# Sample attention of a hybrid decoder step: four sequences' scores side by side on the tensor engine, keys transposed a quarter at a time

## The chip, the core and the metric

One core of a Trainium2 chip runs the whole kernel in one launch. The metric is the device time of a launch in microseconds (us), as the median of three runs. The engines are named as the profile names them: PE is the tensor engine's matrix multiply, PEld its weight load, DVE the vector engine, ACT the scalar engine, POOL the GpSimd engine, and SP the sync engine, which here only issues transfers (DMAs).

## What is computed

One step of a one-layer decoder for a prompt (512 positions) and for a sample group (8 sequences of 8 new positions, with 256 cached positions behind each). The part that matters here is the sample group's windowed attention. It has three head groups with window and dilation (128,1), (512,4) and (2048,16), each with 4 heads of width 64. Cut to the core, the reference does this for each head group, with `q` the normalised queries:

```python
def dilated_cached_attn(q, k_all, v_all, d, n_past):
    T = q.shape[1]
    idx = n_past + jnp.arange(T)[:, None] - d * jnp.arange(BAND + 1)[None, :]
    valid = idx >= 0
    ...
    s = jnp.einsum('bthd,btjhd->bthj', q, kg) * (Dh ** -0.5)
    s = jnp.where(valid[None, :, None, :], s, -jnp.inf)
    m = jnp.max(s, axis=-1, keepdims=True)
    p = jnp.exp(s - m)
    den = jnp.sum(p, axis=-1, keepdims=True)
    o = jnp.einsum('bthj,btjhd->bthd', p / den, vg)
    return o, (m + jnp.log(den))[..., 0]
```

The three groups' results are then merged by softmax weights over their log-denominators. A softmax over all three groups' keys at once gives the same, and that is how the kernel does it: of each sequence it needs 128 keys of the first cache, 256 of the second and 128 of the third (the rows that the dilation can reach), so 512 cached keys, and the new keys behind them.

## The kernel before

**The whole.** The program is a chain of projections on PE with everything else woven between. Each projection is cut into groups: a group of `feat_groups` is 24 matmuls into a tile `pf` (lines 191 to 193), a group of `tok_groups` is 24 matmuls into a tile `ptok` (lines 956 to 958), or 16 for the sample tokens (lines 952 and 953). Weights come in by a DMA from SP into `raw` (line 160), are split by ACT into a high part `wh` (line 138) and by DVE into a low part `wl` (line 139), and go to PE. `Weave.run(main, between)` (line 84) emits the groups of `main` and spreads the steps of the list `between` evenly over the gaps behind them. PE executes in exactly this written order. The orders of DVE, ACT and SP are set by a scheduler when the kernel is built, and each of these engines works through its own list in order: an instruction that waits holds up all that stand behind it.

**The stage of the change.** Line 1023 runs 14 groups (a small low-rank projection, then query, key and value projections of the recurrent branch) with the steps of `sample_steps` between them. Nothing later than this stage reads the sample attention's result before the branches are merged.

**The sample attention.** It works in two halves of four sequences (`half(0)`, `half(1)`). `load_cache` brings a sequence's 512 keys (or values) into a tile `kv` of four quarters of 128 rows x 256 by three DMAs (lines 1296 to 1298: quarter 0, quarters 1 and 2, quarter 3). There are 5 buffers. The steps of a half are:

- `keys(bi)`: loads sequence `bi`'s keys, transposes its 2 x 4 blocks of 128 x 128 on PE into two PSUM tiles `ptk` (line 1311), and copies them to `kTs`, one by DVE and one by ACT (line 1312). `kTs` has 2 buffers.
- `scores(bi)`: the sequence's queries stand in `Qm.Q` as blocks of 32 columns (8 positions x 4 heads). Its scores go to 32 rows of the PSUM tile `psSs`, rows 32*bi and following: six matmuls, two of 256 columns and four of 128 (line 1321). Six more against the new keys go to `psSn` (line 1324). The program puts a matmul of 32 stationary columns on one of four sets of 32 columns of the PE array, by its output rows (0, 32, 64 or 96 and following). So one call of `scores` stays on one set. Behind the fourth sequence follows the softmax of the half: mask additions, maximum, exponential (ACT, line 1334), reciprocal (DVE, line 1335) and scaling (DVE, line 1336) of the tile `Ps`.
- `turn()`: transposes `Ps` (`ptP`, line 1342, and `ptN`, line 1346) and copies it to `PTs` and `PTn`.
- `sums()`: loads the four value tiles and sums the values into `psOs`, one matmul over the new keys (line 1352) and 16 over the cached ones (line 1356). These 16 go around the four column sets: quarter by quarter, and in each quarter sequence by sequence. DVE then masks the sums into `osam` (line 1359).
- `turn_out()`: two small matmuls `ptOs` from `osam` (line 1364), and a split into `aH` and `aL`.

The list of steps that `sample_steps` returns is written by hand:

```python
    return [k0[0], k0[1], s0[0], k0[2], s0[1], k0[3], s0[2], s0[3], k1[0], k1[1], t0, s1[0], k1[2], v0, s1[1],
            k1[3], o0, s1[2], s1[3], rest, rest, t1, rest, v1, rest, o1]
```

Here k, s, t, v and o are keys, scores, turn, sums and turn_out, the digit is the half, and the index is the sequence.

Of the kernel before, what the change touches and what calls it, by code (L numbers as in the profile page):

```python
# [9 lines left out]
F32 = mybir.dt.float32  # L10
# [8 lines left out]
P = 128  # L19
# [881 lines left out]
def sample_masks(E, at):  # L901

    V = E.V
    ms = at.tile([P, NSC], F32, name="msam")
    with E.sb("mka", 2) as wk:
        compare(E, wk, ms[:, 0:128], [[1, 128]], ALU.is_ge, E.p7)
        compare(E, wk, ms[:, 128:384], [[0, 64], [1, 4]], ALU.is_equal, E.p3)
        compare(E, wk, ms[:, 384:512], [[0, 16], [1, 8]], ALU.is_equal, E.p7)
        own = wk.tile([P, 32], F32, tag="own", name="own")
        oth = wk.tile([P, 96], F32, tag="oth", name="oth")  # L910
        compare(E, wk, own, [[1, 4], [0, 8]], ALU.is_equal, E.p5)
        compare(E, wk, oth[:, 0:32], [[0, 4], [1, 8]], ALU.is_le, E.p7)
# [12 lines left out]
    E.ms = ms
# [61 lines left out]
def mixer(E, mxs, bk, xpool, opening):  # L987
# [298 lines left out]
def sample_steps(E, st, Qm):  # L1286

    V, S, G, PE, SP = E.V, E.S, E.G, E.PE, E.SP
    ps_bg, ident = E.ps_bg, E.ident
    wk = st.enter_context(E.sb("samw", 2))  # L1290
    sample_masks(E, Qm.pool)
    cv = [c.rearrange("b r k h d -> b r k (h d)") for c in (E.cache0, E.cache1, E.cache2)]

    def load_cache(b, kv):
        c = wk.tile([P, 4, 256], F32, tag="kv", name="kv", bufs=5)
        SP.dma_start(c[:, 0, :], cv[0][b][:, kv])
        SP.dma_start(c[:, 1:3, :], cv[1][b].rearrange("(c r) k d -> r c k d", r=P)[:, :, kv])
        SP.dma_start(c[:, 3, :], cv[2][b].rearrange("(a r) k d -> a r k d", r=16)[:, 0:8, kv])
        return c

    def half(hf):
        w = SimpleNamespace(k={})
        rn = slice(32 * hf, 32 * hf + 32)

        def keys(bi):
            ck = load_cache(4 * hf + bi, 0)
            w.k[bi] = kTs = wk.tile([P, 2, 512], F32, tag="w4", name="kTs")
            for j in range(2):
                pt = ps_bg("ptk")
                for i in range(4):  # L1310
                    PE.transpose(pt[:, i * P:(i + 1) * P], ck[:, i, j * P:(j + 1) * P], ident)
                (S.copy if j else V.tensor_copy)(kTs[:, j, :], pt)

        def scores(bi):
            b = 4 * hf + bi
            if bi == 0:
                w.S, w.N = ps_bg("psSs"), ps_bg("psSn")
            rr = slice(32 * bi, 32 * bi + 32)
            for (c0, c1, g) in ((0, 128, 0), (128, 384, 1), (384, 512, 2)):
                for j in range(2):  # L1320
                    PE.matmul(w.S[rr, c0:c1], Qm.Q[:, g, j, b, :], w.k[bi][:, j, c0:c1], start=(j == 0), stop=(j == 1))
            for g in range(3):
                for j in range(2):
                    PE.matmul(w.N[rr, g * 32:(g + 1) * 32], Qm.Q[:, g, j, b, :], Qm.K[:, g, j, rn],
                              start=(j == 0), stop=(j == 1))
# [3 lines left out]
            V.tensor_add(Ps[:, :512], w.S, E.ms[:, :512])
# [3 lines left out]
            V.tensor_scalar(st[:, 1:2], st[:, 0:1], -1.0, None, op0=ALU.mult)
            S.activation(Ps, Ps, AF.Exp, bias=st[:, 1:2], accum_out=st[:, 2:3])
            V.reciprocal(st[:, 3:4], st[:, 2:3])
            V.tensor_scalar(Ps, Ps, st[:, 3:4], None, op0=ALU.mult)

        def turn():
            w.T = wk.tile([P, 512], F32, tag="w2", name="PTs")
            pt = ps_bg("ptP")  # L1340
            for i in range(4):
                PE.transpose(pt[:, i * P:(i + 1) * P], w.P[:, i * P:(i + 1) * P], ident)
            S.copy(w.T, pt)
            w.Tn = wk.tile([96, P], F32, tag="PTn", name="PTn", bufs=1)
            pt = ps_bg("ptN")
            PE.transpose(pt[:96, :P], w.P[:, 512:NSC], ident)
            V.tensor_copy(w.Tn, pt[:96, :P])

        def sums():

            po = ps_bg("psOs")
            PE.matmul(po[:, :256], w.Tn, Qm.V[:, hf, :], start=True, stop=False, skip_group_check=True)
            vs = [load_cache(4 * hf + bi, 1) for bi in range(4)]
            for i in range(4):
                for bi in range(4):
                    PE.matmul(po[32 * bi:32 * bi + 32, :256], w.T[:, i * P + bi * 32:i * P + bi * 32 + 32], vs[bi][:, i, :],
                              start=False, stop=(i == 3), skip_group_check=True)
            w.o = wk.tile([P, 256], F32, tag="osam", name="osam")
            V.tensor_mul(w.o, po[:, :256], E.mh)

        def turn_out():
            pt = ps_bg("ptOs")
            for j in range(2):
                PE.matmul(pt[:, 32 * j:32 * j + 32], w.o[:, j * P:(j + 1) * P], E.pick, start=True, stop=True)
            tok = slice(SEQ + 32 * hf, SEQ + 32 * hf + 32)
            E.split(E.aH[:, :, tok], E.aL[:, :, tok], pt[:, 0:64].rearrange("p (j t) -> p j t", j=2))

        f = lambda fn, *a: lambda: fn(*a)
        return [f(keys, b) for b in range(4)], [f(scores, b) for b in range(4)], turn, sums, turn_out

    (k0, s0, t0, v0, o0), (k1, s1, t1, v1, o1) = half(0), half(1)
    rest = lambda: None
    return [k0[0], k0[1], s0[0], k0[2], s0[1], k0[3], s0[2], s0[3], k1[0], k1[1], t0, s1[0], k1[2], v0, s1[1],
            k1[3], o0, s1[2], s1[3], rest, rest, t1, rest, v1, rest, o1]


class Recurrence:
# [349 lines left out]
```

## Time and profile before

| what | us |
|---|---|
| median of 3 runs (lowest, highest) | 1443.35 (1442.48, 1445.37) |
| time of the profiled execution | 1446.7 |
| span of its trace | 1444.2 |
| PE busy | 1414.2 (98% of the span) |
| DVE busy | 1055.3 (73%) |
| ACT busy | 716.7 (50%) |
| the stage of the change, from the first transposed keys to the last `ptOs` | about 629.8 to 700.4 |

The span is the time from the first to the last instruction in the trace; the launch's own time has 2.5 us around it. Rows of the timeline give the start, the time, the engine, the line, the operation, output<-inputs and a count: equal instructions that follow each other are merged in one row, which lasts from the first start to the last end. A float32 matmul shows as two rows of the trace, a transpose as one, so six `scores` matmuls count as x12. Successive PE rows overlap, since a matmul's time includes the way through the array; the pace of PE is read from the distance of the starts.

### The profile page before, as it was taken

What the parts mean: (1) busy time and instruction counts of PE and PEld (TensorE: products, weight loads), DVE (VectorE), ACT (ScalarE), POOL (GpSimd) and SP (SyncE); (2) the same over time, 40 slices, a digit from 0 to 9 for tenths busy, and PEclk for the clock granted to TensorE, in tenths of its full rate; (3) what the DMA queues carried; (4) which work ended last, traced back from release to release, by engine and by line L of the source; (5) the groups of instructions that cost most, each with busy time, mean ns of one, the idle gap of its engine ahead of it and who ended that gap; (6) DMA issues with size and microseconds to landing.
All of it is one profiled execution on the core that took longest, in us unless ns stands there. A gap on an engine that the chain in (4) does not pass through costs nothing.

```text
span 1444.2 us, 27493 instructions
## 1 busy us (share of the span) xinstructions
PE 1414.2 (98%) x10860; PEld 1382.0 (96%) x10860; DVE 1055.3 (73%) x2318; ACT 716.7 (50%) x1458; POOL 66.6 (5%) x105
## 2 busy tenths in 40 slices
PE   7999999999989999999999999999998999999998
PEld 7999999999989999898999999999998999999997
DVE  5999999998845554532576757455579999999882
ACT  6554564665534464622565734223345556556642
POOL 1000000000112211000000000000000000000000
PEclk9999999999999999999999999999999999999999
DMA  7313323332433332274223433235231232333232
GB/s 187 90 43 100 104 84 106 88 103 77 140 107 111 111 120 77 84 204 133 63 74 92 121 110 100 81 95 153 74 88 45 80 111 85 93 104 100 86 106 66
DMA packets 180687, 144.26 MB, mean 100 GB/s; under 512 B 7466, under 2 KB 179168, under 8 KB 180560
## 3 DMA queue, kind: packets, MB, share of 16 engines
q1 hardware_dynamic: 179456, 139.98, 33.4%
q0 software_dynamic: 1104, 2.54, 0.5%
q8 instruction: 85, 1.39, 0.4%
q14 instruction: 42, 0.34, 0.1%
HBM read 128.72 MB, written 13.78 MB: 99 GB/s over the span
## 4 chain that ended last, share of the span: by engine, by line
PE 91%; DVE 5%; DMA 1%; ACT 1%; SPq 1%; issue 0%; POOL 0%; ACTq 0%; POOLq 0%; DVEq 0%
PE pX L545 8%; PE pX L544 7%; PE pX L543 7%; PE pY L545 4%; PE pY L544 4%; PE pY L543 4%; PE pf L191 4%; PE pf L193 3%; PE pf L192 3%; PE ptok L956 3%; PE ptok L958 3%; PE ptok L957 3%; PE pg L191 2%; PE pg L193 2%; PE pg L192 2%; PE pZ L544 2%
## 5 line engine op out<-in xcount | busy, mean ns | idle before, releaser
L138 ACT CAST w<-raw 128x512 fp32r<-128x512 f32 (+1 forms) x348 | 197.9, 577 | 128.5 <-PE pX L545 35.4
L139 DVE TENSOR_TENSOR w<-raw,w 128x512 fp32r<-128x512 f32 (+1 forms) x348 | 215.4, 631 | 18.5 <-ACT w L138 16.3
L138 ACT CAST wh<-raw 128x1024 fp32r<-128x1024 f32 (+2 forms) x115 | 110.7, 972 | 120.2 <-PE pf L192 38.2
L545 PE MATMUL pX<-hop,w 128*128 128x288 f32 x544 | 162.1, 298 | 4.3 <-DVE w L139 4.3
L139 DVE TENSOR_TENSOR wl<-raw,wh 128x1024 fp32r<-128x1024 f32 (+2 forms) x115 | 128.8, 1128 | 49.6 <-ACT wh L138 48.8
L543 PE MATMUL pX<-hop,w 128*128 128x288 f32 x544 | 161.1, 296 | 1.1 <-ACT w L138 0.8
L544 PE MATMUL pX<-hop,w 128*128 128x288 f32 x544 | 161.8, 297 | 0.0
L191 PE MATMUL pf<-h,wh 128*128 128x288 f32 x384 | 120.1, 313 | 3.9 <-ACT wh L138 3.9
L956 PE MATMUL ptok<-wl,h 128*128 128x256 f32 x416 | 120.0, 288 | 0.0
L958 PE MATMUL ptok<-wh,h 128*128 128x256 f32 x416 | 116.7, 281 | 0.0
L957 PE MATMUL ptok<-wh,h 128*128 128x256 f32 x416 | 116.6, 280 | 0.0
L193 PE MATMUL pf<-h,wl 128*128 128x288 f32 x384 | 115.3, 300 | 0.4 <-DVE wl L139 0.4
L192 PE MATMUL pf<-h,wh 128*128 128x288 f32 x384 | 115.3, 300 | 0.0
L545 PEld LDWEIGHTS pX<-hop,w 128*128 128x128 f32 x544 | 103.4, 190 | 5.1 <-DVE w L139 5.1
L543 PEld LDWEIGHTS pX<-hop,w 128*128 128x128 f32 x544 | 103.3, 190 | 1.8 <-ACT w L138 1.2
L544 PEld LDWEIGHTS pX<-hop,w 128*128 128x128 f32 x544 | 103.4, 190 | 0.0
L191 PE MATMUL pg<-h,wh 128*128 128x288 f32 x320 | 97.3, 304 | 2.5 <-ACT wh L138 2.0
L193 PE MATMUL pg<-h,wl 128*128 128x288 f32 x320 | 96.6, 302 | 0.7 <-DVE wl L139 0.7
L192 PE MATMUL pg<-h,wh 128*128 128x288 f32 x320 | 96.9, 303 | 0.0
L191 PEld LDWEIGHTS pf<-h,wh 128*128 128x128 f32 x384 | 74.6, 194 | 7.0 <-ACT wh L138 4.1
L545 PE MATMUL pY<-hop,w 128*128 128x288 f32 x272 | 80.3, 295 | 0.0
L544 PE MATMUL pY<-hop,w 128*128 128x288 f32 x272 | 80.3, 295 | 0.0
(428 smaller groups left out, 4282.9 us busy)
## 6 DMA issues: line engine op xcount, KB each, us to landing
raw<-in_w_in_dram SPq DMA_DIRECT2D x58, 512.0 KB, 4.0
raw<-in_ffn_gate_dram SPq DMA_DIRECT2D x45, 512.0 KB, 3.9
raw<-in_ffn_up_dram SPq DMA_DIRECT2D x44, 512.0 KB, 3.8
raw<-in_ffn_down_dram SPq DMA_DIRECT2D x48, 384.0 KB, 3.2
raw<-in_ffn_down_dram SPq DMA_DIRECT2D x8, 512.0 KB, 3.5
kv<-in_cache_swa_kv_dram SPq DMA_DIRECT2D x32, 128.0 KB, 4.1
kv<-in_cache_swa_kv_dram SPq DMA_DIRECT2D x16, 256.0 KB, 4.4
S<-in_state_gla_dram SPq DMA_DIRECT2D x4, 1024.0 KB, 6.6
```

Of the source, the lines that this page charges most:

```text
L138: S.copy(hi, src)
L139: V.tensor_sub(lo, src, f32(hi))
L191: PE.matmul(ps, h, ah, start=first and j == 0, stop=False)
L192: PE.matmul(ps, h, al, start=False, stop=False)
L193: PE.matmul(ps, l, ah, start=False, stop=last and j == n - 1)
L543: PE.matmul(ps, wh[:, k], ah, start=opens and k == 0, stop=False, skip_group_check=True)
L544: PE.matmul(ps, wh[:, k], al, start=False, stop=False, skip_group_check=True)
L545: PE.matmul(ps, wl[:, k], ah, start=False, stop=k == self.nk - 1, skip_group_check=True)
L956: PE.matmul(po[:, :256], ah, wl, start=(k == 0), stop=False)
L957: PE.matmul(po[:, :256], al, wh, start=False, stop=False)
L958: PE.matmul(po[:, :256], ah, wh, start=False, stop=(k == KD - 1))
```

## The change

The four sequences of a half now go together. `load_cache` is no longer called inside `keys` and `sums`, but by a step `fetch(kv)` that loads all four tiles of a half at once; there are 6 `kv` buffers, and `PTs` has one buffer in place of two. `keys(i)` transposes quarter `i` of all four sequences, again 8 transposes and two copies. `scores(i)` does quarter `i` of all four: 8 matmuls of 128 columns, of which four in a row go to four different column sets. The middle head group's 256 columns are thereby two quarters, so there are 32 such matmuls in a half where there were 24. The 24 matmuls against the new keys come in one piece behind the last quarter, and they go around the column sets too.

The list of steps is new: 31 entries for the same 14 groups. Half 1 begins only after half 0's `o0`, `o0` follows `v0` without a group between, and `t0` and `t1` stand one group behind `s0[3]` and `s1[3]`.

```diff
     def load_cache(b, kv):
-        c = wk.tile([P, 4, 256], F32, tag="kv", name="kv", bufs=5)
+        c = wk.tile([P, 4, 256], F32, tag="kv", name="kv", bufs=6)
...
-        def keys(bi):
-            ck = load_cache(4 * hf + bi, 0)
-            w.k[bi] = kTs = wk.tile([P, 2, 512], F32, tag="w4", name="kTs")
+        def fetch(kv):
+            w.c[kv] = [load_cache(4 * hf + bi, kv) for bi in range(4)]
+
+        def keys(i):
+
+            w.k[i] = kTs = wk.tile([P, 2, 512], F32, tag="w4", name="kTs")
             for j in range(2):
                 pt = ps_bg("ptk")
-                for i in range(4):
-                    PE.transpose(pt[:, i * P:(i + 1) * P], ck[:, i, j * P:(j + 1) * P], ident)
+                for bi in range(4):
+                    PE.transpose(pt[:, bi * P:(bi + 1) * P], w.c[0][bi][:, i, j * P:(j + 1) * P], ident)
                 (S.copy if j else V.tensor_copy)(kTs[:, j, :], pt)
 
-        def scores(bi):
-            b = 4 * hf + bi
-            if bi == 0:
+        def scores(i):
+
+            if i == 0:
                 w.S, w.N = ps_bg("psSs"), ps_bg("psSn")
-            rr = slice(32 * bi, 32 * bi + 32)
-            for (c0, c1, g) in ((0, 128, 0), (128, 384, 1), (384, 512, 2)):
-                for j in range(2):
-                    PE.matmul(w.S[rr, c0:c1], Qm.Q[:, g, j, b, :], w.k[bi][:, j, c0:c1], start=(j == 0), stop=(j == 1))
+            for j in range(2):
+                for bi in range(4):
+                    PE.matmul(w.S[32 * bi:32 * bi + 32, i * P:(i + 1) * P], Qm.Q[:, (0, 1, 1, 2)[i], j, 4 * hf + bi, :],
+                              w.k[i][:, j, bi * P:(bi + 1) * P], start=(j == 0), stop=(j == 1), skip_group_check=True)
+            if i < 3:
+                return
             for g in range(3):
                 for j in range(2):
-                    PE.matmul(w.N[rr, g * 32:(g + 1) * 32], Qm.Q[:, g, j, b, :], Qm.K[:, g, j, rn],
-                              start=(j == 0), stop=(j == 1))
-            if bi < 3:
-                return
+                    for bi in range(4):
+                        PE.matmul(w.N[32 * bi:32 * bi + 32, g * 32:(g + 1) * 32], Qm.Q[:, g, j, 4 * hf + bi, :],
+                                  Qm.K[:, g, j, rn], start=(j == 0), stop=(j == 1), skip_group_check=True)
...
-            w.T = wk.tile([P, 512], F32, tag="w2", name="PTs")
+            w.T = wk.tile([P, 512], F32, tag="w2", name="PTs", bufs=1)
...
-            vs = [load_cache(4 * hf + bi, 1) for bi in range(4)]
+            vs = w.c[1]
...
+    f0(0)
+    return [rest, k0[0], k0[1], s0[0], k0[2], s0[1], k0[3], both(s0[2], lambda: f0(1)), s0[3], rest, t0, rest,
+            both(v0, lambda: f1(0)), o0, rest, rest, rest, k1[0], k1[1], s1[0], k1[2], s1[1], k1[3],
+            both(s1[2], lambda: f1(1)), s1[3], rest, t1, rest, v1, rest, o1]
```

What this makes of the engines' lists shows at three places. In the listings below a row gives the line, the operation, output<-inputs, the output's shape and a count; `pf` and `ptok` rows are the projections' matmuls. First PE in half 0, from the end of one `pf` group to the begin of the next, where the last scores of the half stand. Before:

```order
L193 MATMUL pf<-h_62,wl 128x288
L1321 MATMUL psSs<-kTs,Qm 32x128 x2
L1321 MATMUL psSs<-kTs,Qm 32x256 x2
L1321 MATMUL psSs<-kTs,Qm 32x128 x2
L1324 MATMUL psSn<-KTs,Qm 32x32 x6
L1321 MATMUL psSs<-kTs,Qm 32x128 x2
L1321 MATMUL psSs<-kTs,Qm 32x256 x2
L1321 MATMUL psSs<-kTs,Qm 32x128 x2
L1324 MATMUL psSn<-KTs,Qm 32x32 x6
L191 MATMUL pf<-h_62,wh 128x288
```

And of the change:

```order
L193 MATMUL pf<-h_62,wl 128x288
L1323 MATMUL psSs<-kTs,Qm 32x128 x16
L1330 MATMUL psSn<-KTs,Qm 32x32 x24
L191 MATMUL pf<-h_62,wh 128x288
L192 MATMUL pf<-h_62,wh 128x288
```

Two sequences with all their matmuls became two quarters of all four sequences, and all the half's `psSn` matmuls stand here; the 24 `pf` matmuls that follow are the same, but behind them come `ptP` and `ptN` of half 0 at once, where before came 16 `ptk` and 24 `ptok` matmuls first.

Second, DVE in half 0, from the masks' addition to the copy of `PTn`: `kT` is the evacuation of a `pf` group, `kTs` a copy of transposed keys. Before:

```order
L1329 TENSOR_TENSOR Ps<-psSs,msam 128x512
L1330 TENSOR_TENSOR Ps<-psSn,msam 128x96
L1332 TENSOR_REDUCE st<-Ps 128x1
L1333 TENSOR_SCALAR st<-st 128x1
L1434 TENSOR_TENSOR kT<-pf,row 128x288
L1312 COPY kTs<-ptk 128x512
L1335 RECIPROCAL st<-st 128x1
L1336 TENSOR_SCALAR Ps<-Ps,st 128x608
L1312 COPY kTs<-ptk 128x512
L139 TENSOR_TENSOR wl<-raw,wh 128x1024
L1347 COPY PTn<-ptN 96x128
```

And of the change:

```order
L1333 TENSOR_TENSOR Ps<-psSs,msam 128x512
L1334 TENSOR_TENSOR Ps<-psSn,msam 128x96
L1336 TENSOR_REDUCE st<-Ps 128x1
L1337 TENSOR_SCALAR st<-st 128x1
L1447 TENSOR_TENSOR kT<-pf,row 128x288
L1339 RECIPROCAL st<-st 128x1
L1340 TENSOR_SCALAR Ps<-Ps,st 128x608
L139 TENSOR_TENSOR wl<-raw,wh 128x1024
L1351 COPY PTn<-ptN 96x128
```

Both key copies have left the stretch; the evacuation `kT` still stands ahead of the reciprocal.

Third, PE at the end of half 0's value sums. Before:

```order
L958 MATMUL ptok<-wh,h_62 128x256
L1352 MATMUL psOs<-VAs,PTn 128x256
L1356 MATMUL psOs<-kv,PTs 32x256 x16
L1321 MATMUL psSs<-kTs,Qm 32x128 x2
L1321 MATMUL psSs<-kTs,Qm 32x256 x2
L1321 MATMUL psSs<-kTs,Qm 32x128 x2
L1324 MATMUL psSn<-KTs,Qm 32x32 x6
L956 MATMUL ptok<-wl,h_62 128x256
```

And of the change:

```order
L958 MATMUL ptok<-wh,h_62 128x256
L1356 MATMUL psOs<-VAs,PTn 128x256
L1360 MATMUL psOs<-kv,PTs 32x256 x16
L1368 MATMUL ptOs<-pick,osam 128x32 x2
L956 MATMUL ptok<-wl,h_62 128x256
```

The two `ptOs` matmuls, which read `osam`, now stand directly behind the sums from which DVE makes `osam`; before, a sequence's scores, a `ptok` group and a sequence's transposes stood between.

More of the change, by code (lines that the diff above doesn't have):

```diff
@@ L1301, in half @@
     def half(hf):
-        w = SimpleNamespace(k={})
+        w = SimpleNamespace(k={}, c={})
         rn = slice(32 * hf, 32 * hf + 32)
-        def keys(bi):
-            ck = load_cache(4 * hf + bi, 0)
-            w.k[bi] = kTs = wk.tile([P, 2, 512], F32, tag="w4", name="kTs")
+        def fetch(kv):
+            w.c[kv] = [load_cache(4 * hf + bi, kv) for bi in range(4)]
+        def keys(i):
+            w.k[i] = kTs = wk.tile([P, 2, 512], F32, tag="w4", name="kTs")
             for j in range(2):
                 pt = ps_bg("ptk")
-                for i in range(4):
-                    PE.transpose(pt[:, i * P:(i + 1) * P], ck[:, i, j * P:(j + 1) * P], ident)
+                for bi in range(4):
+                    PE.transpose(pt[:, bi * P:(bi + 1) * P], w.c[0][bi][:, i, j * P:(j + 1) * P], ident)
                 (S.copy if j else V.tensor_copy)(kTs[:, j, :], pt)
-        def scores(bi):
-            b = 4 * hf + bi
-            if bi == 0:
+        def scores(i):
+            if i == 0:
                 w.S, w.N = ps_bg("psSs"), ps_bg("psSn")
-            rr = slice(32 * bi, 32 * bi + 32)
-            for (c0, c1, g) in ((0, 128, 0), (128, 384, 1), (384, 512, 2)):
-                for j in range(2):
-                    PE.matmul(w.S[rr, c0:c1], Qm.Q[:, g, j, b, :], w.k[bi][:, j, c0:c1], start=(j == 0), stop=(j == 1))
+            for j in range(2):
[4 more added lines that the diff above has]
+                return
             for g in range(3):
                 for j in range(2):
-                    PE.matmul(w.N[rr, g * 32:(g + 1) * 32], Qm.Q[:, g, j, b, :], Qm.K[:, g, j, rn],
-                              start=(j == 0), stop=(j == 1))
-            if bi < 3:
-                return
+                    for bi in range(4):
+                        PE.matmul(w.N[32 * bi:32 * bi + 32, g * 32:(g + 1) * 32], Qm.Q[:, g, j, 4 * hf + bi, :],
+                                  Qm.K[:, g, j, rn], start=(j == 0), stop=(j == 1), skip_group_check=True)
             w.P = Ps = wk.tile([P, NSC], F32, tag="Ps", name="Ps", bufs=1)
@@ L1368, in half, with both, g @@
         f = lambda fn, *a: lambda: fn(*a)
-        return [f(keys, b) for b in range(4)], [f(scores, b) for b in range(4)], turn, sums, turn_out
-    (k0, s0, t0, v0, o0), (k1, s1, t1, v1, o1) = half(0), half(1)
+        return [f(keys, b) for b in range(4)], [f(scores, b) for b in range(4)], turn, sums, turn_out, fetch
+    (k0, s0, t0, v0, o0, f0), (k1, s1, t1, v1, o1, f1) = half(0), half(1)
     rest = lambda: None
-    return [k0[0], k0[1], s0[0], k0[2], s0[1], k0[3], s0[2], s0[3], k1[0], k1[1], t0, s1[0], k1[2], v0, s1[1],
-            k1[3], o0, s1[2], s1[3], rest, rest, t1, rest, v1, rest, o1]
+    def both(*steps):
+        def g():
+            for x in steps:
+                x()
+        return g
+    f0(0)
+    return [rest, k0[0], k0[1], s0[0], k0[2], s0[1], k0[3], both(s0[2], lambda: f0(1)), s0[3], rest, t0, rest,
+            both(v0, lambda: f1(0)), o0, rest, rest, rest, k1[0], k1[1], s1[0], k1[2], s1[1], k1[3],
+            both(s1[2], lambda: f1(1)), s1[3], rest, t1, rest, v1, rest, o1]
 class Recurrence:
```

## Prediction

> **What bounds the kernel now.** I read the busy times first, then the stretch of the change by windows, then its timeline. The page says that PE is the bound, and the windows say that this holds in the stage too (columns: stretch, length, busy us and instructions of PE, PEld, DVE, ACT, POOL, then the granted clock, the DMA share and GB/s):
>
> ```profile
> PE 1414.2 (98%) x10860; PEld 1382.0 (96%) x10860; DVE 1055.3 (73%) x2318; ACT 716.7 (50%) x1458; POOL 66.6 (5%) x105
> ```
>
> ```profile
> 625.00:700.00 75.00, 75.00 (x679) 67.51 (x678) 25.54 (x51) 20.28 (x33) 0.98 (x4) 1.00 0.55 159
> ```
>
> From 625 to 700 us PE is busy for 75.00 of 75.00 us at full granted clock; DVE needs 25.54 and ACT 20.28. The list of waits has no PE entry in this stretch. So a microsecond taken out of PE's row here is a microsecond of the kernel, unless PE then has to wait for something that was early so far. The rows of the six places where scores are issued, each with the row that follows (PE's own pace is the distance of starts):
>
> ```profile
> 634.80 1.92 PE L1321 MATMUL psSs<-kTs,Qm 128*32 128x128 f32 x12
> 636.56 0.54 PE L1324 MATMUL psSn<-KTs,Qm 128*32 128x32 f32 x12
> 637.03 1.09 PE L1311 MATMUL ptk<-ident,kv 128*128 128x128 f32 x8
> ...
> 641.25 1.93 PE L1321 MATMUL psSs<-kTs,Qm 128*32 128x128 f32 x12
> ...
> 643.49 1.09 PE L1311 MATMUL ptk<-ident,kv 128*128 128x128 f32 x8
> ...
> 647.67 1.92 PE L1321 MATMUL psSs<-kTs,Qm 128*32 128x128 f32 x12
> ...
> 649.69 0.30 PE L1321 MATMUL psSs<-kTs,Qm 128*32 128x128 f32 x1
> 649.71 0.26 PE L1324 MATMUL psSn<-KTs,Qm 128*32 128x32 f32 x3
> ...
> 651.92 0.40 PE L191 MATMUL pf<-h,wh 128*128 128x288 f32 x1
> ...
> 660.47 1.93 PE L1321 MATMUL psSs<-kTs,Qm 128*32 128x128 f32 x12
> ...
> 662.70 0.39 PE L956 MATMUL ptok<-wl,h 128*128 128x256 f32 x1
> ...
> 669.84 1.93 PE L1356 MATMUL psOs<-kv,PTs 128*32 128x256 f32 x32
> 671.59 1.90 PE L1321 MATMUL psSs<-kTs,Qm 128*32 128x128 f32 x12
> ...
> 673.80 0.38 PE L956 MATMUL ptok<-wl,h 128*128 128x256 f32 x1
> ...
> 680.05 1.92 PE L1321 MATMUL psSs<-kTs,Qm 128*32 128x128 f32 x12
> ...
> 684.30 0.40 PE L191 MATMUL pf<-h,wh 128*128 128x288 f32 x1
> ```
>
> The scores cost PE (637.03 - 634.80) + (643.49 - 641.25) + (651.92 - 647.67) + (662.70 - 660.47) + (673.80 - 671.59) + (684.30 - 680.05) = 2.23 + 2.24 + 4.25 + 2.23 + 2.21 + 4.25 = 17.41 us. In one sequence `psSs` takes 1.76 us (636.56 - 634.80) for 12 rows: 8 of 128 and 4 of 256 columns, 2048 columns, so 0.86 ns a column and 110 ns a 128-column row. `psSn` takes 0.47 us for 12 rows; inside the row they follow each other by (0.54 - 0.20) / 11 = 31 ns, with 0.196 us for one row:
>
> ```profile
> L1324 PE MATMUL psSn<-KTs,Qm x96: 192/196/197, 636.6 to 684.2; 128*32 128x32 f32 x96
> ```
>
> **What four column sets give.** The value sums `psOs` already go around the four sets. Their 32 rows of 256 columns take 671.59 - 669.84 = 1.75 us, 55 ns a row, where one set alone would need 256 x 0.86 = 220. That is four at once to the full. A window of 20 ns shows how: four rows begin together. The prompt's `psO` goes around two sets of 64 columns with rows of 128, the size that the new scores have:
>
> ```profile
> 669.84 0.42 PE L1356 MATMUL psOs<-kv,PTs 128*32 128x256 f32 x4
> 540.18 1.09 PE L1196 MATMUL psO<-PT,VA 128*64 128x128 f32 x16
> ```
>
> ```profile
> L1356 PEld LDWEIGHTS psOs<-kv,PTs x64: 106/110/110, 669.8 to 696.4; 128*32 128x32 f32 x64
> ```
>
> Its rows follow each other by (1.09 - 0.27) / 15 = 55 ns, two in each 110 ns. So the pace of a round is set by its columns, 110 ns at 128, and the sets run in it side by side. The weight loads do not stand in the way: `psOs` has 32 of them in 1.75 us, 55 ns each, although one lasts 110 ns by its row, so they overlap with each other and with the matmuls. The rows at 649.69 and 649.71 show the same on `psSs` and `psSn` themselves: where sequence 2 ends and sequence 3 begins, a `psSs` row of the next set starts ahead of the last three `psSn` rows of the former.
>
> **The change part by part.**
>
> *Scores against the cache.* 32 matmuls a half, 128 rows in all, in rounds of four: 32 rounds x 110 ns = 3.5 us. Bounds: 110 ns by the `psO` rows, 220 ns (7.0 us) if only two sets ran together. I take 110, from the nearest row in size.
>
> *Scores against the new keys.* 96 rows, 24 rounds. No row shows rows of 32 columns on four sets. Lower bound 24 x 31 ns = 0.75 us, upper bound no gain at all, 96 x 31 ns = 3.0 us. I take 0.8: the four starts inside 20 ns at 669.84 say that issuing is not slower than 31 ns for four. With about 0.3 us for the changes between the two kinds the new scores cost 4.6 us. Saved on PE: 17.4 - 4.6 = 12.8 us. The number of places where PE passes from projections to attention work and back stays thirteen, and transposes, copies, value sums and bytes are the same, so these go at nothing; what they would cost moved is 0.1 us a place (`pf` to `psSs` is 0.2 us from start to start, not 0.13).
>
> *The softmax of half 0.* Now `ptP` stands 24 `pf` matmuls behind the last score, and DVE and ACT have just that time. The rows of before:
>
> ```profile
> 651.65 0.69 DVE L1329 TENSOR_TENSOR Ps<-psSs,msam 128x512 f32<-128x512 f32 x1 [3.41 <-PE psSs L1321]
> 653.36 0.15 DVE L1333 TENSOR_SCALAR st<-st 128x1 f32<-128x1 f32 x1
> 653.55 0.80 ACT L1334 ACTIVATE Ps<-Ps,st 128x608 f32<-128x608 f32 x1 [7.00 <-DVE st L1333]
> 654.26 0.18 ACT L1334 ACTIVATION_READ_ACCUMULATOR Ps<-Ps,st 128x1 f32 x1
> 655.10 0.30 PE L193 MATMUL pf<-h,wl 128*128 128x288 f32 x1
> 655.43 0.46 DVE L1434 TENSOR_TENSOR kT<-pf,row 128x288 f32<-128x288 f32 x1 [1.91 <-PE pf L193]
> 655.87 0.69 DVE L1312 COPY kTs<-ptk 128x512 f32<-128x512 f32 x1
> 656.47 0.15 DVE L1335 RECIPROCAL st<-st 128x1 f32<-128x1 f32 x1
> 656.66 0.54 DVE L1336 TENSOR_SCALAR Ps<-Ps,st 128x608 f32<-128x608 f32 x1
> ```
>
> ACT is done at 654.44, but the evacuation `kT` stands ahead of the reciprocal and waits for the last `pf` matmul. So, from that matmul's start: 0.33 to `kT`, 0.44 to the reciprocal (where the key copy began), 0.19 to the scaling, 0.54 for it, about 0.1 until PE starts: 1.6 us. PE would come 0.13 behind its last matmul. New stall: 1.5 us, bounds 1.2 and 2.0. Before, 16 transposes and 24 `ptok` matmuls covered it (PE came to `ptP` only at 659.83, quoted below); that cover is gone.
>
> *The softmax of half 1.* The scheduler put the evacuation ahead of the additions here, so nothing stands between. From the last `psSs` round: 0.33 to the addition, 1.9 to ACT (653.55 - 651.65), 0.9 for ACT, 0.2 and 0.54 on DVE: 3.9 us. PE needs 0.5 for `psSn`, 0.1 and 24 x 0.133 = 3.2 for `pf`: 3.8. Stall 0.1, bounds 0 and 0.4.
>
> *`ptOs` of half 0.* PE now stands until DVE has made `osam`:
>
> ```profile
> 671.92 0.42 DVE L1359 TENSOR_TENSOR osam<-psOs,mh 128x256 f32<-128x256 f32 x1 [4.90 <-PE psOs L1356]
> ```
>
> `osam` is written at 672.34, and PE would start about 0.05 to 0.1 later, at 672.4, in place of 671.59 as it did for the next `psSs`. New stall: 0.8 us, bounds 0.7 and 1.1. Before, a sequence's scores, 24 `ptok` and 8 transposes covered it.
>
> *Transfers.* Half 1's third and fourth key tiles take the buffers of half 0's first two value tiles, which are free when `psOs` ends.
>
> ```profile
> 625.24 0.59 SPq L1296 DMA_DIRECT2D kv<-in_cache_swa_kv_dram  x1
> ...
> 629.79 1.91 PE L1311 MATMUL ptk<-ident,kv 128*128 128x128 f32 x16
> ...
> 656.89 0.36 PE L956 MATMUL ptok<-wl,h 128*128 128x256 f32 x1
> ...
> 659.83 0.60 PE L1342 MATMUL ptP<-ident,Ps 128*128 128x128 f32 x4
> ...
> 671.78 0.34 SPq L1296 DMA_DIRECT2D kv<-in_cache_swa_kv_dram  x1
> ...
> 673.30 0.52 SPq L1296 DMA_DIRECT2D kv<-in_cache_swa_kv_dram  x1
> ...
> 677.60 0.53 PE L1364 MATMUL ptOs<-pick,osam 128*128 128x32 f32 x4
> ```
>
> and from the view of the tile `kv`:
>
> ```profile
> DMA to landing us min/median/max: 1.9/4.3/5.6
> ```
>
> SP issued in the same situation at 671.78 and 673.30. The fourth tile's first quarter is issued 1.5 us behind the first and lands 4.3 later: 5.8 us after `psOs` ends, 7.1 with the longest landing. PE reaches the first transposes of half 1 after the wait for `osam` (672.4 - 671.78 = 0.6), `ptOs` (about 0.4 of its 0.53) and 48 `ptok` matmuls (24 took 659.83 - 656.89 = 2.9): 6.8 us. No stall is the likelier; up to 0.5 in the range. Queued behind these on SP stand value tiles and later weights, which have 10 us and more. At the head, all four key tiles of half 0 must be there at the first transposes (629.79), where before two were enough. The first DMA of the fourth tile was issued at 625.24 and is there 4.3 later, at 629.5. It just fits; up to 0.5.
>
> *Sum.* -12.8 + 1.5 + 0.1 + 0.8 = -10.4 us. The profiled execution took 1446.7 us (span 1444.2), so its like would take 1436.3. That execution lies 3.35 above the median 1443.35; the median should come to 1433.0, 0.7% less.
>
> *A rule against the change.* The rows show loads of 110 ns at a pace of 55 ns (line 1356). The Trainium skill, "TensorE: Matmul & The Clock Gate", Part 3 (Packing small matmuls), states that a weight load overlaps with running matmuls only if the two use different row groups; here every matmul uses all 128 rows, so by that rule each would wait for its load. The trace disagrees at `psOs`, and I go by the trace, with this as a rival.
>
> **The rivals.**
>
> *Issue pace.* If rows on different sets are issued no faster than the 31 ns of `psSn` on one set, `psSs` takes 128 x 31 = 4.0 us and `psSn` 3.0 in place of 3.5 and 0.8: 2.7 us less gain, 1435.7. For it: no row shows a long series below 31 ns, and `psOs` averages 55. Against: four starts in 20 ns. The Trainium skill, same page, Part 1 ("Wait — 56ns, not 53.3ns?"), says that starts never come closer than about 25 ns; by that, as an estimate, `psSn` would take 2.4 us and the kernel 1434.6. Chance 0.13.
>
> *Two sets at once, or late transfers.* Twice the rounds cost 3.5 + 0.8 us: 1437.3. Key tiles late at both places by 1 to 2 us each come to the same region, 1435 to 1437. Against: `psOs`, and the sums above. Chance 0.08.
>
> *No overlap at all.* The four sets write one PSUM tile; if that made them take turns, 128 x 110 ns + 96 x 31 ns + 0.3 = 17.4 us is what there was, and the new stalls of 2.4 stay: 1445.8, no measurable change. Against: `psOs` is one tile too. Chance 0.04.
>
> *Slower: loads laid bare.* If the load of a row could not begin before the row ahead on another set was through, every one of the 224 rows would take the 110 ns of its load: 24.6 us, 7.2 more than the 17.4 of now, and with 2.4 of stalls 1453.0. The kernel gets slower from (17.4 - 2.4) / 224 = 67 ns a row. Against: `psOs` at 55 ns a row. This is what the rule of the Trainium skill above would make of the change. Chance 0.04.
>
> **How the numbers follow.** The forecast has a chance of 0.71, with a range of its own of 1430.5 (hardly a stall) to 1435 (all stalls at their upper bounds). The range over all reaches from 1430.0 (the whole 13.2 us that the lower bounds give) to 1438.5 (two sets at once, plus 1 us of late transfers), and leaves out the last two rivals. Runs of this kernel differ by some 0.2%, 2.9 us, which is what a measurement can tell from no change: all of the forecast and the first two rivals lie below 1440.5. Faster 0.71 + 0.13 + 0.08 = 0.92, same 0.04, slower 0.04.
>
> **What would show it.** Right: `psSs` of a quarter as 16 rows in about 0.46 us from start to start; `psSs` x32 and `psSn` x48 of the last two quarters in 1.4; a PE wait of about 1.5 us at `ptP` for DVE's `Ps` in half 0 and one of 0.8 at `ptOs` for `osam`, and no other in the stage; the stage shorter by 10 us and the rest unchanged. Wrong: `psSs` rows at 110 ns each; PE waiting for a `kv` transfer at `ptk`; a later stage that waits where it did not, so that the 10 us are given back.

## The result, and the profile after

| | median us | executions | ratio to the kernel before, 95% interval |
|---|---|---|---|
| before | 1443.21 | 1440.05 to 1445.37 and one of 7767.32, 8 of them | 1 |
| changed | 1431.09 | 1430.26 to 1438.25, 8 of them | 0.9931 [0.9917, 0.9946] |

The change makes the kernel faster by 0.7%. The ratio is worth 10.0 us, between 7.8 and 12.0, and the forecast of -10.4 lies inside that. The two medians differ by 12.1.

The profiled executions differ by more, 1446.7 - 1430.5 = 16.2 us, and most of what is over has nothing to do with the change. The cores' view gives the span and the mean granted clock, first of the kernel before, then of the changed one, then of a second profile of the same changed kernel (`after_again` below):

```profile
core 0: 1444.2 us, clock 0.987
```

```profile
core 0: 1428.7 us, clock 0.993
```

```profile
core 0: 1430.7 us, clock 0.990
```

Spans follow the clock. So the stage of the change is read by itself, from the start of the first `ptk` row to the start of the last `ptOs` row; the granted clock in it was 1.00 in each profile. Before, that was 700.17 - 629.79 = 70.38 us. After, PE's timeline in the stage reads (start, us, line, output<-inputs, count, in brackets the idle time ahead and its releaser):

```profile
627.94 1.91 PE L1314 MATMUL ptk<-ident,kv 128*128 128x128 f32 x16
...
632.95 0.64 PE L1323 MATMUL psSs<-kTs,Qm 128*32 128x128 f32 x16
633.52 1.09 PE L1314 MATMUL ptk<-ident,kv 128*128 128x128 f32 x8
...
637.75 0.64 PE L1323 MATMUL psSs<-kTs,Qm 128*32 128x128 f32 x16
638.32 1.09 PE L1314 MATMUL ptk<-ident,kv 128*128 128x128 f32 x8
...
642.51 1.08 PE L1323 MATMUL psSs<-kTs,Qm 128*32 128x128 f32 x32
643.41 0.64 PE L1330 MATMUL psSn<-KTs,Qm 128*32 128x32 f32 x48
643.97 0.40 PE L191 MATMUL pf<-h,wh 128*128 128x288 f32 x1
...
648.72 0.63 PE L1346 MATMUL ptP<-ident,Ps 128*128 128x128 f32 x4 [1.28 <-DVE Ps L1340]
...
652.64 1.93 PE L1360 MATMUL psOs<-kv,PTs 128*32 128x256 f32 x32
655.20 0.63 PE L1368 MATMUL ptOs<-pick,osam 128*128 128x32 f32 x4 [0.62 <-DVE osam L1363]
...
661.38 1.04 PE L1314 MATMUL ptk<-ident,kv 128*128 128x128 f32 x8
...
679.15 0.66 PE L1346 MATMUL ptP<-ident,Ps 128*128 128x128 f32 x4
...
688.62 0.53 PE L1368 MATMUL ptOs<-pick,osam 128*128 128x32 f32 x4
```

The stage lasts 688.62 - 627.94 = 60.68 us, 9.70 less than before; in the second profile it was 60.67. Half 0's scores cost PE (633.52 - 632.95) + (638.32 - 637.75) + (643.97 - 642.51) = 0.57 + 0.57 + 1.46 = 2.60 us, and half 1's, summed in the same way, 2.61: together 5.2, where 17.4 stood. Two waits are new, and these two only: 1.28 us ahead of `ptP` in half 0 and 0.62 ahead of its `ptOs`. The `ptP` of half 1 at 679.15 and the first key transposes of half 1 at 661.38 carry no bracket, so nothing was waited for there.

The page and the windows show the same from afar. PE is still the bound:

```profile
PE 1395.4 (98%) x10892; PEld 1366.0 (96%) x10892; DVE 1054.5 (74%) x2318; ACT 714.2 (50%) x1458; POOL 66.6 (5%) x105
```

```profile
625.00:690.00 65.00, 63.09 (x710) 57.87 (x709) 24.70 (x46) 20.29 (x35) 0.98 (x4) 1.00 0.61 176
```

In the stage PE is busy for 63.09 of 65.00 us, where before it was for all of 75.00: the idle 1.91 are the two waits.

What PE stands for at `ptP` is seen on ACT and DVE, as in the rows of before. The last row of the exponential on ACT:

```profile
646.26 0.19 ACT L1338 ACTIVATION_READ_ACCUMULATOR Ps<-Ps,st 128x1 f32 x1
```

and DVE behind it:

```profile
647.48 0.46 DVE L1447 TENSOR_TENSOR kT<-pf,row 128x288 f32<-128x288 f32 x1 [1.96 <-PE pf L193]
647.85 0.15 DVE L1339 RECIPROCAL st<-st 128x1 f32<-128x1 f32 x1
648.04 0.54 DVE L1340 TENSOR_SCALAR Ps<-Ps,st 128x608 f32<-128x608 f32 x1
```

ACT is through at 646.45. The reciprocal starts only at 647.85, behind the evacuation `kT`, for which DVE itself had stood 1.96 us, until PE's last `pf` matmul was done. That it is the place behind `kT`, and not the length of the two steps, which delays `ptP` is read from these rows; no run moved `kT` alone.

### The profile page after: what moved, and what is told of

The parts are those of the page before. It is cut to its first block, busy times and chain, and to the rows that moved or that the text cites. A ratio compares the mean times of both kernels' runs of the same rounds, so it can differ in the third digit from the quotient of the medians.

```text
span 1428.7 us, 27553 instructions
## 1 busy us (share of the span) xinstructions
PE 1395.4 (98%) x10892; PEld 1366.0 (96%) x10892; DVE 1054.5 (74%) x2318; ACT 714.2 (50%) x1458; POOL 66.6 (5%) x105
## 4 chain that ended last, share of the span: by engine, by line
PE 89%; DVE 5%; ACT 2%; DMA 2%; issue 1%; SPq 1%; POOL 0%; ACTq 0%; POOLq 0%; DVEq 0%
PE pX L545 8%; PE pX L544 8%; PE pX L543 7%; PE pY L544 4%; PE pY L545 4%; PE pY L543 4%; PE pf L191 4%; PE pf L193 4%; PE pf L192 3%; PE ptok L956 3%; PE ptok L958 3%; PE ptok L957 3%; PE pZ L544 2%; PE pZ L545 2%; PE pZ L543 2%; PE pg L193 2%
## 5 line engine op out<-in xcount | busy, mean ns | idle before, releaser
L139 DVE TENSOR_TENSOR w<-raw,w 128x512 fp32r<-128x512 f32 (+1 forms) x348 | 215.9, 632 | 19.0 <-ACT w L138 17.4
```

The lines of the kernel that those rows point to most:

```text
L139: V.tensor_sub(lo, src, f32(hi))
```

## The experiments

In all of them the stage's length is the fine measure: two profiles of one kernel gave 60.68 and 60.67, while the medians carry intervals of some 0.2% to each side, 2 to 4 us. The second and third columns are the starts of the first `ptk` row and of the last `ptOs` row in each profile.

| kernel | first `ptk` | last `ptOs` | stage us | median us | ratio to before, 95% interval |
|---|---|---|---|---|---|
| before | 629.79 | 700.17 | 70.38 | 1440.43 to 1443.21 (medians beside the others) | 1 |
| changed | 627.94 | 688.62 | 60.68 | 1431.09 | 0.9931 [0.9917, 0.9946] |
| after_again | 627.00 | 687.67 | 60.67 | 1431.59 | 0.9947 [0.9927, 0.9967] |
| e_serial | 625.73 | 687.94 | 62.21 | 1433.15 | 0.9947 [0.9930, 0.9964] |
| e_pairs | 623.88 | 684.70 | 60.82 | 1430.33 | 0.9929 [0.9902, 0.9956] |
| e_psn_serial | 626.23 | 688.39 | 62.16 | 1433.74 | 0.9945 [0.9928, 0.9962] |
| e_seq_keys | 624.82 | 684.36 | 59.54 | 1429.70 | 0.9927 [0.9902, 0.9952] |
| e_run8 | 623.90 | 688.11 | 64.21 | 1434.61 | 0.9961 [0.9946, 0.9976] |
| e_run28 | 623.90 | 695.40 | 71.50 | 1444.47 | 1.0027 [1.0013, 1.0042] |
| e_defer_norm | 624.81 | 684.05 | 59.24 | 1429.35 | 0.9930 [0.9904, 0.9956] |
| e_o0_later | 626.08 | 686.12 | 60.04 | 1429.80 | 0.9932 [0.9908, 0.9957] |
| e_both | 625.60 | 684.11 | 58.51 | 1429.94 | 0.9923 [0.9902, 0.9945] |
| e_best | 627.15 | 684.48 | 57.33 | 1427.14 | 0.9908 [0.9890, 0.9927] |

The theory at the start: the gain is that four column sets run side by side, and two new waits take some of it back. Its rival: the gain comes from the rest of the change, the new list, the early loads, the transposes by quarters.

**e_serial.** The rows of one set issued one behind the other.

```diff
-            for j in range(2):
-                for bi in range(4):
+            for bi in range(4):
+                for j in range(2):
                     PE.matmul(w.S[32 * bi:32 * bi + 32, i * P:(i + 1) * P], ...
...
-            for g in range(3):
-                for j in range(2):
-                    for bi in range(4):
+            for bi in range(4):
+                for g in range(3):
+                    for j in range(2):
                         PE.matmul(w.N[32 * bi:32 * bi + 32, g * 32:(g + 1) * 32], ...
```

> The changed kernel with its list of steps, loads, quarter-wise transposes and all other instructions, but the rows of a column set issued one behind the other (sequence as the outer loop) in psSs and in psSn. Theory (the gain is that four sets run side by side): a quarter of 16 psSs rows takes 16 x 110 ns = 1.76 us in place of 0.57, eight of them +9.5 us; 48 psSn rows take 1.5 us in place of 0.56, two of them +1.9; so +11.4 us against the changed kernel, about 1442.5. Rival (the gain comes from the other list, the early loads or the transposes by quarters): no difference, about 1431.

PE's timeline at the second quarter, and at the end of the scores of half 0:

```profile
635.56 0.66 PE L1323 MATMUL psSs<-kTs,Qm 128*32 128x128 f32 x16
636.15 1.09 PE L1314 MATMUL ptk<-ident,kv 128*128 128x128 f32 x8
...
641.24 1.38 PE L1330 MATMUL psSn<-KTs,Qm 128*32 128x32 f32 x48
642.55 0.40 PE L191 MATMUL pf<-h,wh 128*128 128x288 f32 x1
```

The theory fell for `psSs`. A quarter still takes 0.59 us, not 1.76, although the 4 rows of a set now follow each other (a matmul makes two rows). For `psSn`, where the run of a set is 12 rows, 48 rows take 642.55 - 641.24 = 1.31 us in place of 643.97 - 643.41 = 0.56. The stage is 1.53 longer than in the changed kernel, nearly all of it (2 x 0.75) from `psSn`.

**e_pairs.** Sequences 0 and 1 for both `j`, then 2 and 3.

```diff
-            for j in range(2):
-                for bi in range(4):
+            for bi, j in ((0, 0), (1, 0), (0, 1), (1, 1), (2, 0), (3, 0), (2, 1), (3, 1)):
+                if True:
                     PE.matmul(w.S[32 * bi:32 * bi + 32, i * P:(i + 1) * P], ...
```

> The changed kernel with psSs going around two sets only at a time (sequences 0 and 1, then 2 and 3); psSn unchanged. Theory (sets run side by side, a round takes the time of its columns, 110 ns): 16 rows in 8 rounds, 0.88 us in place of 0.57, +0.31 in eight places, +2.5 us against the changed kernel, about 1433.6. Rival (the pace of 0.57 us for 16 rows is that of issuing, whatever the sets): 0.57 us a quarter, no difference, about 1431.

```profile
633.70 0.66 PE L1323 MATMUL psSs<-kTs,Qm 128*32 128x128 f32 x16
634.29 1.09 PE L1314 MATMUL ptk<-ident,kv 128*128 128x128 f32 x8
```

0.59 us again, and the stage 0.14 longer: no loss, against the theory as it was put. But 0.59 us for 16 rows, 37 ns a row, isn't the rival's pace of issuing either: `psSn` has 48 rows in 0.56 us in the changed kernel, 12 ns a row.

**e_psn_serial.** The second half of e_serial's edit alone, `psSn` set by set, `psSs` as changed.

> The changed kernel with the psSn rows alone put back to one set after the other. Theory (the sets' gain holds for rows of 32 columns too): 48 rows take 48 x 31 ns = 1.5 us in place of 0.56, +0.9 in two places, +1.9 us against the changed kernel, about 1433.0. Rival (rows this small are issued at one pace whatever the sets): no difference, about 1431.

The stage is 62.16 us, 1.48 longer, 0.74 in each half (expected 0.9). Together with e_serial's 1.53 this says that set-by-set order costs for `psSn`, with 12 rows a run, and next to nothing for `psSs`, with 4. The two kinds of row differ in their columns as well, so that it is the run's length is shown only by e_run8 below, which lengthens the runs of `psSs`.

**The theory, mended.** PE takes the rows in their order, but not as strictly as the section on the kernel before says: it can begin a row of another set while a few rows of the set ahead still wait. Runs of 4 rows lie within that reach, so their order doesn't matter; a run of 12 holds the next set up. Before the change a run was a whole sequence, 24 rows, and most sequences stood apart from the next by other work. Three kernels test that.

**e_seq_keys.** Keys transposed per sequence as before, all scores of a half in one block over the four sets. `kTs` has four buffers; to make room, `kv` has four, and the value loads are issued behind the last key transposes.

```diff
-            w.k[i] = kTs = wk.tile([P, 2, 512], F32, tag="w4", name="kTs")
+            w.k[i] = kTs = wk.tile([P, 2, 512], F32, tag="w4", name="kTs", bufs=4)
...
-                for bi in range(4):
-                    PE.transpose(pt[:, bi * P:(bi + 1) * P], w.c[0][bi][:, i, j * P:(j + 1) * P], ident)
+                for r in range(4):
+                    PE.transpose(pt[:, r * P:(r + 1) * P], w.c[0][i][:, r, j * P:(j + 1) * P], ident)
...
+            if i < 3:
+                return
+            w.S, w.N = ps_bg("psSs"), ps_bg("psSn")
+            for r in range(4):
+                for j in range(2):
+                    for bi in range(4):
+                        PE.matmul(w.S[32 * bi:32 * bi + 32, r * P:(r + 1) * P], Qm.Q[:, (0, 1, 1, 2)[r], j, 4 * hf + bi, :],
+                                  w.k[bi][:, j, r * P:(r + 1) * P], start=(j == 0), stop=(j == 1), skip_group_check=True)
```

> The changed kernel with keys transposed sequence by sequence, as before, into four kTs buffers (kv then has four buffers in place of six, and the value loads are issued one step earlier), and all scores of a half issued in one place over the four sets. Theory (only the order of the score rows matters): 32 psSs rows and 48 psSn rows a set of four go as fast as in the changed kernel, some 2.5 us a half; about 1431, from 1430 to 1432.5 if a value tile comes late with four buffers. Rival (the transposes by quarters are needed for the gain): above 1435.

```profile
637.94 1.96 PE L1325 MATMUL psSs<-kTs,Qm 128*32 128x128 f32 x64
639.71 0.64 PE L1330 MATMUL psSn<-KTs,Qm 128*32 128x32 f32 x48
640.28 0.40 PE L191 MATMUL pf<-h,wh 128*128 128x288 f32 x1
```

64 `psSs` rows take 639.71 - 637.94 = 1.77 us, 27.7 ns a row, which is a quarter of 110: four at once without a loss. The half's scores take 2.34 us, less than the 2.60 of the changed kernel, since PE passes to them once and not three times, and the stage is 1.14 shorter. So the transposes by quarters aren't needed for the gain. What the two kernels have in common is that the four sequences' scores are issued in one place and in turn.

**e_run8 and e_run28.** e_seq_keys with longer runs of one set, 8 `psSs` rows, and then a whole sequence with its 16 `psSs` and 12 `psSn` rows.

```diff
-            for r in range(4):
-                for j in range(2):
-                    for bi in range(4):
+            for h in range(2):
+                for bi in range(4):
+                    for r, j in ((2 * h, 0), (2 * h, 1), (2 * h + 1, 0), (2 * h + 1, 1)):
```

> e_seq_keys (all scores of a half in one block) with psSs issued in runs of 8 rows of one set, then 8 of the next, twice around; psSn unchanged. Theory formed on e_serial and e_psn_serial (rows are issued in their order and PE starts a row of another set only from among the next 3 or so; runs of 4 rows lie within that reach, runs of 12 don't): a set's run holds up the next for 8 - 3 = 5 rows, 7 x 5 x 110 ns + 8 x 110 ns = 4.7 us for the 64 rows in place of 1.77, the six places together 10.6 us in place of 4.7, about 5.9 us slower than e_seq_keys, stage 65.7 us. Rival (the order inside a block does not matter, only that the rows of all sets are issued in one place): 1.77 us, no difference to e_seq_keys.

```diff
-            for r in range(4):
-                for j in range(2):
-                    for bi in range(4):
+            for bi in range(4):
+                for r in range(4):
+                    for j in range(2):
                         PE.matmul(w.S[32 * bi:32 * bi + 32, r * P:(r + 1) * P], ...
-            for g in range(3):
-                for j in range(2):
-                    for bi in range(4):
+                for g in range(3):
+                    for j in range(2):
                         PE.matmul(w.N[32 * bi:32 * bi + 32, g * 32:(g + 1) * 32], ...
```

> e_seq_keys with the rows of one sequence in one run, as before the change: 16 psSs rows, then its 12 psSn rows, then the next sequence, still in one block. Theory (reach of about 3 rows): a set holds up the next for 16 x 110 + 9 x 31 ns = 2.04 us, 3 x 2.04 + 2.13 = 8.3 us a half, 16.5 us in place of 4.7, 11.9 us slower than e_seq_keys, stage about 71.7 us: the gain is gone although the new list, loads and buffers stay. Rival (order inside a block does not matter): no difference to e_seq_keys, stage 59.8.

PE's timeline of e_run8 in half 0:

```profile
637.02 4.00 PE L1325 MATMUL psSs<-kTs,Qm 128*32 128x128 f32 x61
640.75 0.26 PE L1330 MATMUL psSn<-KTs,Qm 128*32 128x32 f32 x6
640.86 0.38 PE L1325 MATMUL psSs<-kTs,Qm 128*32 128x128 f32 x2
...
641.08 0.27 PE L1325 MATMUL psSs<-kTs,Qm 128*32 128x128 f32 x1
641.18 0.59 PE L1330 MATMUL psSn<-KTs,Qm 128*32 128x32 f32 x36
641.70 0.40 PE L191 MATMUL pf<-h,wh 128*128 128x288 f32 x1
```

The half's scores take 641.70 - 637.02 = 4.68 us, 2.34 more than in e_seq_keys, so the stage is 4.67 longer. Expected were 5.9: the order inside a block matters, and the size was counted one row too high. If a run of 8 holds the next up for 4 rows and not 5, `psSs` takes 7 x 4 x 110 + 8 x 110 ns = 3.96 us, and with the 0.57 of `psSn` that is 4.5. The rows say the same: the first `psSn` rows, which are on other sets, begin at 640.75, behind 61 of the 64 `psSs` rows, with three of the last run still to come.

The beginning of e_run28's scores in half 0:

```profile
637.02 1.94 PE L1325 MATMUL psSs<-kTs,Qm 128*32 128x128 f32 x16
638.79 0.45 PE L1329 MATMUL psSn<-KTs,Qm 128*32 128x32 f32 x9
639.05 0.30 PE L1325 MATMUL psSs<-kTs,Qm 128*32 128x128 f32 x1
639.08 0.26 PE L1329 MATMUL psSn<-KTs,Qm 128*32 128x32 f32 x3
639.18 1.80 PE L1325 MATMUL psSs<-kTs,Qm 128*32 128x128 f32 x15
...
641.08 0.30 PE L1325 MATMUL psSs<-kTs,Qm 128*32 128x128 f32 x1
...
645.34 0.40 PE L191 MATMUL pf<-h,wh 128*128 128x288 f32 x1
```

This shows the reach within one sequence's scores. The first row of the second sequence starts at 639.05, right behind the ninth of the first sequence's 12 `psSn` rows, with three still to come. So a run of n rows holds the next up by n - 4 rows' paces, which is what e_run8 has too. A sequence takes 639.05 - 637.02 = 2.03 us (expected 2.04, and 16 x 110 + 8 x 31 ns = 2.01 by n - 4), and the next one too (641.08 - 639.05). The half's scores take 645.34 - 637.02 = 8.32 us. The stage is 71.50 us (expected 71.7), 12.0 more than in e_seq_keys and 10.8 more than in the changed kernel, and the ratio is 1.0027 [1.0013, 1.0042]: the whole gain is gone while the early loads and the calls that gather a half's scores in one block stay. The rival, that everything else made the gain, is out.

**e_defer_norm.** The scaling by the reciprocal moves from `Ps` to `osam`.

```diff
-            V.tensor_scalar(Ps, Ps, st[:, 3:4], None, op0=ALU.mult)
+            w.r = st[:, 3:4]
...
-            V.tensor_mul(w.o, po[:, :256], E.mh)
+            V.scalar_tensor_tensor(w.o, po[:, :256], w.r, E.mh, op0=ALU.mult, op1=ALU.mult)
```

> The changed kernel without the scaling of Ps by the reciprocal of its sum; the reciprocal is applied where osam is made, in the multiplication that is there anyway. ptP then waits for ACT's exponential alone. Theory (half 0's wait at ptP is the reciprocal and the scaling queued behind the evacuation kT on DVE): the wait of 1.28 us at ptP goes, -1.5 us against the changed kernel, about 1429.6. Rival (another wait follows at once, PTs or kv): the time stays at 1431.

```profile
644.15 0.60 PE L1346 MATMUL ptP<-ident,Ps 128*128 128x128 f32 x4
...
650.66 0.63 PE L1368 MATMUL ptOs<-pick,osam 128*128 128x32 f32 x4 [0.69 <-DVE osam L1363]
```

`ptP` stands for nothing, and the stage is 60.68 - 59.24 = 1.44 us shorter, as the theory said. The wait at `ptOs` is 0.07 longer. The ratio, 0.9930 [0.9904, 0.9956], can't tell that from no difference.

**e_o0_later.** `ptOs` of half 0 one slot later.

```diff
-            both(v0, lambda: f1(0)), o0, rest, rest, rest, k1[0], k1[1], s1[0], k1[2], s1[1], k1[3],
+            both(v0, lambda: f1(0)), rest, o0, rest, rest, k1[0], k1[1], s1[0], k1[2], s1[1], k1[3],
```

> The changed kernel with ptOs of half 0 one slot later in the list of steps, behind 24 ptok matmuls. Theory (PE stands at ptOs because osam is made from the psOs just ended): the wait of 0.62 us goes and 0.7 to 0.8 us are gained, about 1430.3; half 1's first key transposes come 0.7 us earlier against their loads, which had 1.8 us to spare, and still don't wait. Rival (PE then waits for the kv transfer instead): 1431.

```profile
655.62 0.53 PE L1368 MATMUL ptOs<-pick,osam 128*128 128x32 f32 x4
```

The wait is gone, and the stage is 0.64 shorter (expected 0.7 to 0.8).

**e_both.** The edits of e_defer_norm and e_o0_later together.

> Both edits, the scaling moved to osam and ptOs of half 0 one slot later. Theory (the two waits are independent): -2.3 us against the changed kernel, about 1428.8, PE without a wait in the stage. But half 1's first key transposes come 0.8 us earlier against loads that are issued when psOs ends, with 1.8 us to spare: no wait. Rival (the gains do not add, a transfer becomes the wait): about 1430.

The stage is 58.51 us, 2.17 shorter (1.44 + 0.64 = 2.08): the two gains add up. The window shows PE without a gap:

```profile
625.00:690.00 65.00, 65.00 (x730) 60.53 (x729) 24.89 (x47) 22.53 (x41) 0.98 (x4) 1.00 0.60 173
```

**e_best.** The edits of e_both made to e_seq_keys.

> e_seq_keys with both edits for the waits: the scaling of Ps moved to osam, ptOs of half 0 one slot later. Theory (the three gains are independent): stage 59.8 - 1.4 - 0.6 = 57.8 us, 3.1 us less than in the changed kernel, about 1428. Rival (with four kv buffers a transfer becomes the wait at the first key transposes of half 1): stage 58.5 to 59.5.

```profile
657.92 1.04 PE L1314 MATMUL ptk<-ident,kv 128*128 128x128 f32 x8
...
684.48 0.53 PE L1368 MATMUL ptOs<-pick,osam 128*128 128x32 f32 x4
```

The stage is 57.33 us, 3.35 shorter than in the changed kernel and 13.05 shorter than before. Half 1's first transposes don't wait although `kv` has four buffers. The median is 1427.14 and the ratio 0.9908 [0.9890, 0.9927]. On the same chip the changed kernel had 0.9947 [0.9927, 0.9967]; this version is the fastest of all here.

**after_again.** The changed kernel, unaltered.

> The changed kernel once more, on the same chip as the others, to see how far the median and the stage differ from execution to execution. The stage's length should be 60.7 us again to 0.1; the median 1431 with some 0.2% of scatter.

60.67 us for the stage, and 1431.59.

## Why the prediction was right

**The mechanism.** Side by side on four sets: shown. e_run28 issues the same 224 rows in one place, sequence by sequence, and takes 2 x 8.32 = 16.6 us for them; the changed kernel takes 5.2, and e_seq_keys, with the rows in the other order and all else alike, 4.7.

**The scores' cost, 4.6 us.** It was 5.2, so 12.2 saved in place of 12.8. The pace of a round was right: within a block it is 27.7 ns a row, 110 a round (e_seq_keys). Two sizes were short. The four quarters that stand alone cost 0.57 us each for 16 rows where 0.46 was forecast, since PE's passing to another kind of matmul is paid six times; issued in two blocks the scores cost 2 x 2.34 = 4.7. `psSn` costs 0.56 us a half, 1.12 together, between the bounds of 0.75 and 3.0 but 0.3 above the value taken (0.8).

**`ptP` of half 0, 1.5 us.** 1.28 idle on PE, 1.44 by removal. The reason fits the rows: reciprocal and scaling stand behind an evacuation that waits for PE's own last matmul.

**`ptP` of half 1, 0.1.** No wait was seen.

**`ptOs` of half 0, 0.8.** The prediction meant by this how much later PE comes to the row behind the value sums. From the start of the 32 `psOs` rows that is 655.20 - 652.64 = 2.56 us, where before it was 671.59 - 669.84 = 1.75: 0.81, as forecast. The idle time that the profile shows is 0.62, and moving `ptOs` away gains 0.64, just below the lower bound of 0.7.

**Transfers, none.** Right. The first DMA of half 1's fourth key tile on SP's queue, and the landing times of the tile `kv`:

```profile
656.10 0.53 SPq L1296 DMA_DIRECT2D kv<-in_cache_swa_kv_dram  x1
```

```profile
DMA to landing us min/median/max: 2.1/4.2/5.0
```

Even the longest landing, 5.0, is over at 661.1, and the transposes start at 661.38. It is close; e_o0_later reaches them 0.6 us sooner behind the sums, and still doesn't wait.

**The sum.** -12.2 + 1.44 + 0.81 + 0 = -9.9, and the stage became 9.70 shorter; the 0.2 left are not traced here. The forecast was -10.4: 0.6 us of the saving were missing, and 0.15 less of waiting (2.25 in place of 2.4) made up for a part. By the stage alone the median would be 1443.2 - 9.7 = 1433.5. The measured 1431.09 lies 2.4 below that and 1.9 below the forecast of 1433.0, both within the scatter of the medians of before (1440.43 to 1443.35 here). That the ratio's 10.0 comes so close to 10.4 is in part luck, since its interval is 2 us wide to each side. The lower end of the forecast's range, 1430.5, went beyond the prediction's own bounds: with the least two stalls, 1.2 + 0.7, and the whole 13.2 saved, they give 1443.35 - 13.2 + 1.9 = 1432.1.

**The rivals.** Issue pace: out. Four `psSs` rows of four sets lie in a window of 20 ns:

```profile
642.51 0.32 PE L1323 MATMUL psSs<-kTs,Qm 128*32 128x128 f32 x4
```

and the 48 `psSn` rows of the changed kernel go at 0.56 / 48 = 12 ns a row, well below 31. The Trainium skill, "TensorE: Matmul & The Clock Gate", Part 1 ("Wait — 56ns, not 53.3ns?"), has starts never closer than about 25 ns; for rows on different column sets these rows, four starts in 20 ns, differ. Two sets at once: out by the 27.7 ns a row, four in 110; e_pairs couldn't show it, since runs that short overlap in any order. No overlap at all, and loads laid bare: out, by the loads of e_seq_keys' `psSs` rows (shortest, median and longest in ns):

```profile
L1325 PEld LDWEIGHTS psSs<-kTs,Qm x128: 106/110/110, 637.9 to 670.8; 128*32 128x32 f32 x128
```

A half's 64 rows go at 27.7 ns each, although a load lasts 110 ns, and all of them use the 128 rows of the array. So what the Trainium skill, "TensorE: Matmul & The Clock Gate", Part 3 (Packing small matmuls), says of loads and row groups doesn't hold here for rows on different column sets. The kernel before could have told as much even for one set, where `psSn` rows follow each other by 31 ns with loads of 110 to 114:

```profile
L1324 PEld LDWEIGHTS psSn<-KTs,Qm x96: 110/113/114, 636.5 to 684.1; 128*32 128x32 f32 x96
```

**What the prediction overlooked.** It quoted that a `psSs` row starts ahead of the last three `psSn` rows of the sequence before it, and read this only as a sign that sets overlap. It was also the size of PE's reach, and so the reason why the order inside a quarter doesn't matter. For want of that, e_serial was expected to lose 11.4 us and lost 1.5. Why the reach is three rows, no run here shows.

## What to carry to other kernels

Small matmuls on different column sets ran side by side here where PE met them within a few rows of each other. Gather them in one place, in runs of at most four rows of a set (two float32 matmuls), and don't scatter them over the program in blocks of one set each; a finer alternation gave next to nothing more (0.57 us against 0.59 for 16 rows). When a shorter PE row takes away the cover of a softmax chain, look at what stands ahead of the chain's last small steps on DVE, and move a scaling behind the product where it can ride on an operation that is there anyway.

## What the runs showed of the hardware

- The reach: PE begins a row of another column set while three rows of the set ahead are still to come, but not sooner (e_run8, e_run28). Against alternating rows, runs of 4 rows cost 0.02 us on 16 rows, runs of 8 cost 2.34 us on the 64 `psSs` rows of a half, and runs of a whole sequence, 28 rows, 8.32 - 2.34 = 5.98 us on its 112 rows of scores. Runs of 5 to 7 rows were not measured.
- Rows of 32 columns on four sets are faster by less than four: from the first start to the last, 48 rows of the changed kernel's `psSn` go at (0.64 - 0.20) / 47 = 9.4 ns a row, 3.3 times as fast as the 31 ns on one set, which is read in the same way.
- The places where PE passes to another kind of matmul add up: e_seq_keys, with two blocks of scores in place of six, has a stage 1.14 us shorter, 2 x (2.60 - 2.34) = 0.5 of it in the scores' own rows.
- Outside the stage the kernel's length follows the mean granted clock: 1444.2 - 70.38 = 1373.8 us at 0.987, 1370.0 at 0.990 (after_again), 1368.0 at 0.993 (changed). The shortest is e_run8's, 1427.8 - 64.21 = 1363.6 at 0.995. e_o0_later fits in with 1434.8 - 60.04 = 1374.8 at 0.987:

```profile
core 0: 1434.8 us, clock 0.987
```
